# One tile for all slabs, paired transfers of slabs 1+2 and 4+5, and tables through ScalarE's ring in a rotary-embedding kernel

## The chip, the cores and the metric

The kernel runs on one core of one Trainium2 chip. The core has TensorE (matmul), VectorE, ScalarE and GpSimd as compute engines, SyncE, and 16 DMA engines that move data between the device memory (HBM) and the on-chip memory (SBUF, 128 partitions). Each engine works through its own list of instructions in order; an instruction may wait for a semaphore that another engine or a transfer raises. The metric is the time of one execution on the device in microseconds (us), as the median over several executions.

## What is computed

A rotary position embedding. `x` has 16 batches, 512 positions and 1024 values, which are 16 heads of 64; `cos` and `sin` are 512 x 32. All are float32, and the output is 16 x 512 x 16 x 64 in float32.

```python
x = x.reshape(batch, seq, num_heads, head_dim)
x1, x2 = x[..., :half_dim], x[..., half_dim:]
cos = cos[None, :, None, :]
sin = sin[None, :, None, :]
rotated = np.concatenate([
    x1 * cos - x2 * sin,
    x1 * sin + x2 * cos
], axis=-1)
```

Input and output are 33.55 MB each.

## The kernel before

The work is cut into eight slabs of two batches. A slab is 1024 rows of 1024 values, laid on 128 partitions with 8 rows each (`rpp`): 32 KB of float32 per partition (`W` = 8192 values), 4.19 MB in all. One load on SyncE's queue (line 62) brings a slab in; five slab buffers (`slots`) exist, and slab s + 5 is loaded into the buffer of slab s once slab s has been stored. A load of a full slab is 128 rows of 32 KB that are spread over the 16 DMA engines, so each gets 8.

A slab goes through these steps, whole for slabs 1 to 5 and in two halves (passes of four rows per partition) for slabs 0, 6 and 7:

- ScalarE casts it to bfloat16 into `xb` (line 119; two such buffers).
- VectorE multiplies `xb` by the sin table into `t2`, which lies in the first half of the slab's own buffer (line 140), multiplies `xb` by the cos table in place (line 140 again), and adds the two with the halves of each head exchanged (line 143).
- ScalarE casts the sum back to float32 into the slab's buffer (line 146).
- ScalarE issues the store from its own queue (line 158 for slabs 0 to 6; slab 7 is stored in two halves by line 155).

The code asks for the cast of the next pass before the work of the present one. The order on each engine is settled when the program is built. Before the change, ScalarE's order is: casts of slab 0 (two halves), cast of slab 1, both casts back of slab 0, store 0, cast 2, back 1, store 1, cast 3, back 2, store 2, and so on; VectorE finishes one slab's three operations before it begins the next slab's, except that the two halves of slab 0 overlap by one.

The tables are made at the start. Two GpSimd-issued transfers (line 73) bring `cos` and `sin` to 128 partitions, four positions each, in one tile `raw`. GpSimd casts it to bfloat16 (line 98) and builds selection matrices of 1 and -1 (`pick`, lines 89 to 92); eight matmuls (line 104) spread the four-position rows to the eight rows of each partition and sign the sin half; VectorE casts the result from PSUM to `tab` (line 110). VectorE's first multiply needs `tab` and the first cast.

Loads 1 to 4 carry a hand-made dependency on the cos transfer: SyncE issues them only when it has landed. Slab 7's second half has a hand-made order behind the issue of its first half.

Of the kernel before, what the change touches and what calls it, by code (L numbers as in the profile page):

```python
# [2 lines left out]

# [4 lines left out]


@with_exitstack  # L10
def kernel(
    ctx: ExitStack,
    tc: tile.TileContext,
    x: bass.AP,
    cos: bass.AP,
    sin: bass.AP,
    num_heads: int,
    out: bass.AP,
):
    nc = tc.nc  # L20
    P = nc.NUM_PARTITIONS

    batch, seq, dim = x.shape
    nh = num_heads
    hd = dim // nh
    half = hd // 2
    bf16 = mybir.dt.bfloat16
    f32 = mybir.dt.float32

    nb = 2  # L30
    slots = 5
    nslabs = batch // nb
    rpp = nb * seq // P
    W = rpp * dim
    SP = seq // rpp
    TW = rpp * half

    out_flat = out.rearrange("b s h d -> b s (h d)")

    singles = ctx.enter_context(tc.tile_pool(name="singles", bufs=1))  # L40
    slabs = ctx.enter_context(tc.tile_pool(name="slabs", bufs=slots))
    xpool = ctx.enter_context(tc.tile_pool(name="xpool", bufs=2))
    psum = ctx.enter_context(tc.tile_pool(
        name="psum", bufs=1, space=bass.MemoryType.PSUM))


    def dram(t, s, a=0, n=W):
        return bass.AP(tensor=t.tensor, offset=t.offset + s * nb * seq * dim + a,
                       ap=[[W, P], [1, n]])


    def view(t, offset, *dims):
        return dataclasses.replace(t, offset=t.offset + offset,
                                   ap=[t.ap[0], *[list(d) for d in dims]])


    slab = {}


    def load(s):  # L60
        slab[s] = slabs.tile([P, W], f32, tag="slab", name="slab")
        return nc.sync.dma_start(out=slab[s], in_=dram(x, s))  # L62


    load(0)


    TR = seq // P
    G = rpp // TR
    table = {}  # L70
    raw = singles.tile([P, 2 * TR * half], f32, tag="raw")
    for i, src in enumerate((cos, sin)):
        table[i] = nc.gpsimd.dma_start(out=view(raw, i * TR * half, (1, TR * half)), in_=bass.AP(  # L73
            tensor=src.tensor, offset=src.offset,
            ap=[[TR * half, P], [1, TR * half]]))

    for s in range(1, slots):
        tc.add_manual_dep(  # L80
            load(s).ins, table[0].ins.name,
            mybir.DependencyInfo(mybir.DependencyClass.Sync,
                                 mybir.DependencyReason.DATA),
            reason="issue")

    pick = singles.tile([P, 2 * G * P], bf16, tag="pick")
    nc.gpsimd.memset(pick, 0.0)  # L89
    for g in range(2 * G):  # L90
        part = view(pick, g * P, (SP, P // SP), (1, SP))
        nc.gpsimd.affine_select(  # L92
            out=part, in_=part, compare_op=mybir.AluOpType.not_equal,
            fill=1.0 if g < G else -1.0, base=-(g % G),
            pattern=[[0, P // SP], [-G, SP]], channel_multiplier=1)

    tab1 = singles.tile([P, 2 * TR * half], bf16, tag="tab1")
    nc.gpsimd.tensor_copy(out=tab1, in_=raw)  # L98

    acc = psum.tile([P, 2 * rpp * hd], f32, tag="acc")  # L100
    for i in range(2):
        for h in range(2):
            for g in range(G):
                nc.tensor.matmul(  # L104
                    view(acc, (i * rpp + g * TR) * hd + h * half, (hd, TR), (1, half)),
                    view(pick, (i * h * G + g) * P, (1, P)),
                    view(tab1, i * TR * half, (half, TR), (1, half)),
                    start=True, stop=True)
    tab = singles.tile([P, 2 * rpp * hd], bf16, tag="tab")
    nc.vector.tensor_copy(out=tab, in_=acc)  # L110

    xb = {}


    def cast(u):
        s, r, n = u
        if r == 0:
            xb[s] = xpool.tile([P, W], bf16, tag="xb", name="xb")
        nc.scalar.copy(out=view(xb[s], r * dim, (1, n * dim)),  # L119
                       in_=view(slab[s], r * dim, (1, n * dim)))  # L120

    passes = []
    for s in range(nslabs):
        n = rpp if 1 <= s < nslabs - 2 else rpp // 2
        passes += [(s, r, n) for r in range(0, rpp, n)]


    cast(passes[0])
    for i, (s, r, n) in enumerate(passes):
        if i + 1 < len(passes):
            cast(passes[i + 1])
        xs = view(slab[s], r * dim, (1, n * dim))
        xu = view(xb[s], r * dim, (1, n * dim))

        t2 = view(slab[s].bitcast(bf16), 2 * r * dim, (1, n * dim))
        for t, a in ((t2, rpp * hd), (xu, 0)):
            nc.vector.tensor_mul(  # L140
                out=t, in0=xu,
                in1=view(tab, a + r * hd, (hd, n), (0, nh), (1, hd)))
        nc.vector.tensor_add(  # L143
            out=xu, in0=xu, in1=view(t2, half, (hd, n * nh), (-half, 2), (1, half)))

        back = nc.scalar.copy(out=xs, in_=xu)  # L146
        if s == nslabs - 1:

            if r > 0:
                tc.add_manual_dep(  # L150
                    back.ins, part.ins.name,
                    mybir.DependencyInfo(mybir.DependencyClass.NoSync,
                                         mybir.DependencyReason.DATA),
                    reason="issue")
            part = nc.scalar.dma_start(
                out=dram(out_flat, s, r * dim, n * dim), in_=xs)
        elif r + n == rpp:
            nc.scalar.dma_start(out=dram(out_flat, s), in_=slab[s])  # L158
            if s + slots < nslabs:
                load(s + slots)  # L160


# [1 line left out]
_INS = ['x', 'cos', 'sin', 'num_heads']  # L164
_OUTS = [((16, 512, 16, 64), 'float32')]

_NUMBERS = {'num_heads': 16}


# [26 lines left out]
```

## Time and profile before

| | us |
|---|---|
| median of 10 runs (162.25 to 162.75) | 162.44 |
| the profiled execution | 162.48 |
| its span, first to last instruction | 160.7 |
| ScalarE busy | 113.5 |
| VectorE busy | 108.5 |
| cast of a whole slab, ScalarE (line 119) | 7.02 |
| cast back of a whole slab, ScalarE (line 146) | 7.01 |
| each cast of half a slab, ScalarE | 3.60 |
| each VectorE operation on a whole slab (lines 140, 143) | 4.42 |
| each VectorE operation on half a slab | 2.29 |
| load of a slab, issue to landing, median of 8 | 24.1 |
| store of a slab, issue to landing, median of 7 | 28.3 |
| cos and sin, issue to landing | 6.9 and 8.9 |

The span is 1.8 us shorter than the time of the same execution: some time lies around the instructions. The profile tells when each instruction ran, what it waited for, and how busy the 16 DMA engines were; "DMA share" is their mean busy share. Of 67.24 MB moved, 33.69 MB are read from HBM and 33.55 MB written to it. SyncE's queue took 49.3% and ScalarE's 48.4% of the DMA engines' time over the span; GpSimd's took 0.2%.

### The profile page before, as it was taken

The page shows a single profiled execution, that of the slowest core. Times are in us where ns is not written, and L with a number is a line of the kernel's source. Part 1 is how long each engine was busy: PE and PEld are TensorE (multiplying, and loading weights), DVE is VectorE, ACT ScalarE, POOL GpSimd, SP SyncE. Part 2 cuts the span into 40 slices and gives each one's busy share as a digit, 9 for nine tenths or more (in the row PEclk, how much of TensorE's full clock was granted, in tenths as well). Part 3 has the DMA queues.
Part 4 walks back from the last instruction along what each step waited for, and adds up shares of the span by engine and source line. Part 5 has one row for each costly group of instructions (what it writes and reads, how often), then busy time and mean ns, then how long its engine had stood idle before and what let it go on. Part 6 is the DMA issues. An engine that isn't in the chain of part 4 may idle for free.

```text
span 160.7 us, 169 instructions
## 1 busy us (share of the span) xinstructions
PE 1.0 (1%) x8; PEld 0.8 (1%) x8; DVE 108.5 (68%) x34; ACT 113.5 (71%) x23; POOL 3.4 (2%) x12
## 2 busy tenths in 40 slices
PE   0010000000000000000000000000000000000000
PEld 0010000000000000000000000000000000000000
DVE  0003799999899979997995199939469599900000
ACT  3007939998998999899909995199995999280000
POOL 7000000000000000000000000000000000000000
DMA  7999999999999999999999999999999999999994
GB/s 261 408 408 408 506 392 400 506 400 392 383 400 465 440 400 416 489 400 408 498 400 408 498 400 400 506 400 400 498 408 392 489 424 392 473 432 400 416 432 196
DMA packets 2512, 67.24 MB, mean 418 GB/s; under 512 B 304, under 2 KB 304, under 8 KB 336
## 3 DMA queue, kind: packets, MB, share of 16 engines
q1 hardware_dynamic: 1152, 33.55, 49.3%
q10 hardware_dynamic: 1296, 33.56, 48.4%
q0 software_dynamic: 64, 0.13, 0.2%
HBM read 33.69 MB, written 33.55 MB: 418 GB/s over the span
## 4 chain that ended last, share of the span: by engine, by line
DMA 49%; ACT 30%; issue 6%; DVE 4%; ACTq 0%; SPq 0%; POOLq 0%
DMA slab<-in_x_dram 24%; DMA out_dram<-slab 21%; ACT slab L146 16%; ACT xb L119 14%; DMA raw<-in_cos_dram 4%; DVE xb L143 1%; DVE xb L140 1%; DVE slab L140 1%; ACTq L158 0%; SPq L62 0%; POOLq L177 0%
## 5 line engine op out<-in xcount | busy, mean ns | idle before, releaser
L119 ACT CAST xb<-slab 128x4096 bf16<-128x4096 f32 (+1 forms) x11 | 56.6, 5155 | 26.8 <-DMA slab<-in_x_dram 25.6
L146 ACT CAST slab<-xb 128x4096 f32<-128x4096 bf16 (+1 forms) x11 | 56.6, 5153 | 3.4 <-DVE xb L143 3.4
L140 DVE TENSOR_TENSOR slab<-xb,tab 128x4096 bf16<-128x4096 bf16 (+1 forms) x11 | 35.9, 3260 | 19.3 <-ACT xb L119 19.2
L143 DVE TENSOR_TENSOR xb<-xb,slab 128x4096 bf16<-128x4096 bf16 (+1 forms) x11 | 35.9, 3261 | 0.3
L140 DVE TENSOR_TENSOR xb<-xb,tab 128x4096 bf16<-128x4096 bf16 (+1 forms) x11 | 35.9, 3261 | 0.3
L110 DVE CAST tab<-acc 128x1024 bf16<-128x1024 f32 x1 | 1.2, 1225 | 12.4 <-PE acc L104 12.4
L119 ACT ACT_TABLE_LOAD x1 | 1.3, 1283 | 0.7 <-PEq L177 0.7
L104 PE MATMUL acc<-tab,pick 128*128 128x128 bf16 x8 | 1.0, 308 | 11.3 <-POOL tab L98 11.3
L92 POOL TENSOR_SCALAR_AFFINE_SELECT pick<-pick 128x128 bf16<-128x128 bf16 x4 | 1.0, 288 | 0.1
L104 PEld LDWEIGHTS <-pick 128*128 128x128 bf16 x8 | 0.8, 140 | 11.2 <-issue 7.8
L73 POOL DMA_DIRECT2D raw<-in_cos_dram x1 | 0.7, 674 | 0.8 <-POOLq L177 0.8
L89 POOL MEMSET pick<- 128x512 bf16 x1 | 0.5, 543 | 0.0
L98 POOL CAST tab<-raw 128x256 bf16<-128x256 f32 x1 | 0.4, 396 | 6.8 <-DMA raw<-in_sin_dram 6.8
L73 POOL DMA_DIRECT2D raw<-in_sin_dram x1 | 0.5, 534 | 0.0
L177 POOL MEMSET const-float32-0.0<- 128x1 f32 x1 | 0.1, 99 | 0.2 <-issue 0.2
L177 POOL MEMSET const-bfloat16-1.0<- 128x1 bf16 x1 | 0.1, 102 | 0.0
L177 POOL MEMSET const-uint8-127<- 128x1 uint8 x1 | 0.1, 102 | 0.0
L177 POOL MEMSET const-float32-1.0<- 128x1 f32 x1 | 0.1, 99 | 0.0
## 6 DMA issues: line engine op xcount, KB each, us to landing
slab<-in_x_dram SPq DMA_DIRECT2D x8, 4096.0 KB, 24.1
out_dram<-slab ACTq DMA_DIRECT2D x7, 4096.0 KB, 28.3
out_dram<-slab ACTq DMA_DIRECT2D x2, 2048.0 KB, 16.2
raw<-in_cos_dram POOLq DMA_DIRECT2D x1, 64.0 KB, 6.9
raw<-in_sin_dram POOLq DMA_DIRECT2D x1, 64.0 KB, 8.9
```

Source lines behind the costliest of these rows:

```text
L73: table[i] = nc.gpsimd.dma_start(out=view(raw, i * TR * half, (1, TR * half)), in_=bass.AP(tensor=src.tensor, offset=src.offset, ap=[[TR * ...
L89: nc.gpsimd.memset(pick, 0.0)
L92: nc.gpsimd.affine_select(out=part, in_=part, compare_op=mybir.AluOpType.not_equal, fill=1.0 if g < G else -1.0, base=-(g % G), pattern=[[ ...
L98: nc.gpsimd.tensor_copy(out=tab1, in_=raw)
L104: nc.tensor.matmul(view(acc, (i * rpp + g * TR) * hd + h * half, (hd, TR), (1, half)), view(pick, (i * h * G + g) * P, (1, P)), view(tab1, ...
L110: nc.vector.tensor_copy(out=tab, in_=acc)
L119: nc.scalar.copy(out=view(xb[s], r * dim, (1, n * dim)), in_=view(slab[s], r * dim, (1, n * dim)))
L140: nc.vector.tensor_mul(out=t, in0=xu, in1=view(tab, a + r * hd, (hd, n), (0, nh), (1, hd)))
L143: nc.vector.tensor_add(out=xu, in0=xu, in1=view(t2, half, (hd, n * nh), (-half, 2), (1, half)))
L146: back = nc.scalar.copy(out=xs, in_=xu)
L177: nc = _bacc.Bacc("TRN2", target_bir_lowering=False, num_devices=1)
```

## The change

- The five slab buffers become one tile `mem` of five slots. Slab s lies in slot (s + 1) mod 5: slab 0 in slot 1, slabs 1 and 2 in slots 2 and 3, slab 3 in slot 4, slab 4 in slot 0, slab 5 in slot 1.
- Slabs 1 and 2 are loaded by one transfer of 8.39 MB. Slabs 4 and 5 are stored by one transfer of 8.39 MB, issued after slab 5's cast back.
- The last slab is stored by one transfer, after its second half.
- Tables: `cos` and `sin` go to 64 partitions, eight positions (1 KB) each, in two tiles, issued by ScalarE ahead of its other work. GpSimd casts each on its own; four matmuls instead of eight spread and sign them.
- Loads 1 to 4 no longer wait for the cos transfer.

```diff
--- before.py
+++ after.py
@@ -38,15 +38,9 @@
     out_flat = out.rearrange("b s h d -> b s (h d)")
 
     singles = ctx.enter_context(tc.tile_pool(name="singles", bufs=1))
-    slabs = ctx.enter_context(tc.tile_pool(name="slabs", bufs=slots))
     xpool = ctx.enter_context(tc.tile_pool(name="xpool", bufs=2))
     psum = ctx.enter_context(tc.tile_pool(
         name="psum", bufs=1, space=bass.MemoryType.PSUM))
-
-
-    def dram(t, s, a=0, n=W):
-        return bass.AP(tensor=t.tensor, offset=t.offset + s * nb * seq * dim + a,
-                       ap=[[W, P], [1, n]])
 
 
     def view(t, offset, *dims):
@@ -54,58 +48,65 @@
                                    ap=[t.ap[0], *[list(d) for d in dims]])
 
 
-    slab = {}
 
 
-    def load(s):
-        slab[s] = slabs.tile([P, W], f32, tag="slab", name="slab")
-        return nc.sync.dma_start(out=slab[s], in_=dram(x, s))
+    mem = singles.tile([P, slots * W], f32, tag="mem")
+
+
+    def at(s):
+        return (s + 1) % slots * W
+
+
+
+    def dram(t, s, n):
+        return bass.AP(tensor=t.tensor, offset=t.offset + s * nb * seq * dim,
+                       ap=[[W, P], [nb * seq * dim, n], [1, W]])
+
+
+    def sbuf(s, n):
+        return view(mem, at(s), (W, n), (1, W))
+
+
+    def load(s, n=1):
+        nc.sync.dma_start(out=sbuf(s, n), in_=dram(x, s, n))
 
 
     load(0)
 
 
-    TR = seq // P
-    G = rpp // TR
-    table = {}
-    raw = singles.tile([P, 2 * TR * half], f32, tag="raw")
-    for i, src in enumerate((cos, sin)):
-        table[i] = nc.gpsimd.dma_start(out=view(raw, i * TR * half, (1, TR * half)), in_=bass.AP(
-            tensor=src.tensor, offset=src.offset,
-            ap=[[TR * half, P], [1, TR * half]]))
+    cos_sb = singles.tile([SP, TW], f32, tag="cos_sb")
+    sin_sb = singles.tile([SP, TW], f32, tag="sin_sb")
+    for t, src in ((cos_sb, cos), (sin_sb, sin)):
+        nc.scalar.dma_start(out=t, in_=bass.AP(
+            tensor=src.tensor, offset=src.offset, ap=[[TW, SP], [1, TW]]))
+
+    load(1, 2)
+    for s in range(3, slots):
+        load(s)
 
 
 
-    for s in range(1, slots):
-        tc.add_manual_dep(
-            load(s).ins, table[0].ins.name,
-            mybir.DependencyInfo(mybir.DependencyClass.Sync,
-                                 mybir.DependencyReason.DATA),
-            reason="issue")
-
-
-
-    pick = singles.tile([P, 2 * G * P], bf16, tag="pick")
+    pick = singles.tile([SP, 2 * P], bf16, tag="pick")
     nc.gpsimd.memset(pick, 0.0)
-    for g in range(2 * G):
+    for g in range(2):
         part = view(pick, g * P, (SP, P // SP), (1, SP))
         nc.gpsimd.affine_select(
             out=part, in_=part, compare_op=mybir.AluOpType.not_equal,
-            fill=1.0 if g < G else -1.0, base=-(g % G),
-            pattern=[[0, P // SP], [-G, SP]], channel_multiplier=1)
+            fill=1.0 - 2.0 * g, base=0, pattern=[[0, P // SP], [-1, SP]],
+            channel_multiplier=1)
 
-    tab1 = singles.tile([P, 2 * TR * half], bf16, tag="tab1")
-    nc.gpsimd.tensor_copy(out=tab1, in_=raw)
+    tab1 = singles.tile([SP, 2 * TW], bf16, tag="tab1")
+    for i, t in enumerate((cos_sb, sin_sb)):
+        nc.gpsimd.tensor_copy(out=view(tab1, i * TW, (1, TW)), in_=t)
 
     acc = psum.tile([P, 2 * rpp * hd], f32, tag="acc")
     for i in range(2):
         for h in range(2):
-            for g in range(G):
-                nc.tensor.matmul(
-                    view(acc, (i * rpp + g * TR) * hd + h * half, (hd, TR), (1, half)),
-                    view(pick, (i * h * G + g) * P, (1, P)),
-                    view(tab1, i * TR * half, (half, TR), (1, half)),
-                    start=True, stop=True)
+            nc.tensor.matmul(
+                view(acc, i * rpp * hd + h * half, (hd, rpp), (1, half)),
+                view(pick, i * h * P, (1, P)),
+                view(tab1, i * TW, (half, rpp), (1, half)),
+                start=True, stop=True)
     tab = singles.tile([P, 2 * rpp * hd], bf16, tag="tab")
     nc.vector.tensor_copy(out=tab, in_=acc)
 
@@ -117,7 +118,7 @@
         if r == 0:
             xb[s] = xpool.tile([P, W], bf16, tag="xb", name="xb")
         nc.scalar.copy(out=view(xb[s], r * dim, (1, n * dim)),
-                       in_=view(slab[s], r * dim, (1, n * dim)))
+                       in_=view(mem, at(s) + r * dim, (1, n * dim)))
 
 
 
@@ -132,10 +133,10 @@
     for i, (s, r, n) in enumerate(passes):
         if i + 1 < len(passes):
             cast(passes[i + 1])
-        xs = view(slab[s], r * dim, (1, n * dim))
+        xs = view(mem, at(s) + r * dim, (1, n * dim))
         xu = view(xb[s], r * dim, (1, n * dim))
 
-        t2 = view(slab[s].bitcast(bf16), 2 * r * dim, (1, n * dim))
+        t2 = view(mem.bitcast(bf16), 2 * (at(s) + r * dim), (1, n * dim))
         for t, a in ((t2, rpp * hd), (xu, 0)):
             nc.vector.tensor_mul(
                 out=t, in0=xu,
@@ -143,19 +144,13 @@
         nc.vector.tensor_add(
             out=xu, in0=xu, in1=view(t2, half, (hd, n * nh), (-half, 2), (1, half)))
 
-        back = nc.scalar.copy(out=xs, in_=xu)
-        if s == nslabs - 1:
+        nc.scalar.copy(out=xs, in_=xu)
+        if r + n == rpp:
 
-            if r > 0:
-                tc.add_manual_dep(
-                    back.ins, part.ins.name,
-                    mybir.DependencyInfo(mybir.DependencyClass.NoSync,
-                                         mybir.DependencyReason.DATA),
-                    reason="issue")
-            part = nc.scalar.dma_start(
-                out=dram(out_flat, s, r * dim, n * dim), in_=xs)
-        elif r + n == rpp:
-            nc.scalar.dma_start(out=dram(out_flat, s), in_=slab[s])
+            if s != 4:
+                first, count = (4, 2) if s == 5 else (s, 1)
+                nc.scalar.dma_start(out=dram(out_flat, first, count),
+                                    in_=sbuf(first, count))
             if s + slots < nslabs:
                 load(s + slots)
```

In the changed program as built, ScalarE's order is: the two table issues, two half casts of slab 0, two half casts back, store 0, cast 1, cast 2, back 1, store 1, cast 3, back 2, store 2, cast 4, back 3, store 3, cast 5, back 4, two half casts of slab 6, back 5, store 4 and 5, first half back of 6, first half cast of 7, second half back of 6, second half cast of 7, store 6, two halves back of 7, store 7. VectorE's first multiply of slab 2 stands ahead of slab 1's add, and both first multiplies of slab 6's halves ahead of its others. SyncE's list is load 0, loads 1 and 2, 3, 4, and then 5, 6 and 7, which wait for stores 0, 1 and 2.

## The prediction

> **What bounds the kernel now.** I read the page's busy rows and its DMA row first, then the stretches by time, then the chain of waits, then the rows by shape for durations.
>
> ```profile
> PE 1.0 (1%) x8; PEld 0.8 (1%) x8; DVE 108.5 (68%) x34; ACT 113.5 (71%) x23; POOL 3.4 (2%) x12
> DMA  7999999999999999999999999999999999999994
> DMA 49%; ACT 30%; issue 6%; DVE 4%; ACTq 0%; SPq 0%; POOLq 0%
> ```
>
> No compute engine is above 71%, while the DMA row is at 9 in 38 of 40 slices. The chain names transfers for only 49%, but a chain follows one releaser at a time. The stretches show the resource itself:
>
> ```profile
> 0.00:1.70 1.70, 0.00 (x0) 0.00 (x0) 0.00 (x0) 0.96 (x1) 0.67 (x5) 1.00 0.00 0
> 2.00:36.00 34.00, 1.01 (x8) 0.85 (x8) 20.27 (x9) 20.20 (x6) 2.39 (x7) 1.00 0.99 424
> 36.00:44.00 8.00, 0.00 (x0) 0.00 (x0) 7.62 (x2) 7.55 (x2) 0.00 (x0) 1.00 1.01 389
> 66.00:100.00 34.00, 0.00 (x0) 0.00 (x0) 27.75 (x7) 27.88 (x4) 0.00 (x0) 1.00 1.00 433
> 100.00:158.00 58.00, 0.00 (x0) 0.00 (x0) 32.42 (x14) 35.36 (x9) 0.00 (x0) 1.00 1.00 430
> ```
>
> The last two columns are the DMA share and GB/s. From 1.7 us to the end the share is 1.0 for loads alone, loads with stores, and stores alone. So the kernel takes the time its bytes need, and anything that leaves the transfer engines without queued work for a moment is paid in full. One 4.19 MB slab costs 4.194 / 0.4325 = 9.70 us (slabs 1's and 0's casts start 22.93 - 13.22 = 9.71 us apart, each released by its load). The stretch 36 to 44, where the first store begins, is slower: 8 x (1 - 389/430) = 0.8 us lost. The last store is issued at 144.54 and lands 15.0 us later, at 159.5, 1.2 us before the end of the span.
>
> What keeps the queue filled is ScalarE and VectorE, which hand out stores early enough:
>
> ```profile
> 16.86 2.29 DVE L140 TENSOR_TENSOR slab<-xb,tab 128x4096 bf16<-128x4096 bf16 x1 [3.24 <-ACT xb L119]
> 28.11 2.29 DVE L143 TENSOR_TENSOR xb<-xb,slab 128x4096 bf16<-128x4096 bf16 x1
> 29.85 7.11 ACT L146 CAST slab<-xb 128x4096 f32<-128x4096 bf16 x2
> 36.99 0.38 ACTq L158 DMA_DIRECT2D out_dram<-slab  x1
> 51.38 0.34 ACTq L158 DMA_DIRECT2D out_dram<-slab  x1
> 65.72 0.34 ACTq L158 DMA_DIRECT2D out_dram<-slab  x1
> ```
>
> Stores come every 65.72 - 51.38 = 14.34 us when ScalarE is not starved (cast 7.02, cast back 6.93, issue 0.4). A slab needs 2 x 9.70 = 19.4 us of transfer, so ScalarE has slack, but only as long as each store is issued when its own slab is done.
>
> **What the Trainium skill says.** "DMA: Bandwidth & Descriptors", section "Issuing engines are not separate DMA queues": transfers issued by different engines run on the same 16 DMA engines and interleave. The trace agrees: two queues together reach 430 to 433 GB/s, one alone 430. So moving the tables to ScalarE's queue buys no bandwidth. Section "Why a DMA increments its semaphore by 16 and not by 1" says that the number of engines is the largest divisor up to 16 of the slowest dimension: 64 rows still use all 16, four rows each; no run here shows it yet. Section "Queues, rings and completion order" says that each DMA engine takes turns between queues by packet; the cos table in the trace landed 6.9 us after its issue though it is 64 KB, which fits waiting behind slab packets. The section on the increment by 16 also says that only the full count means that all data has landed, and a paired load has one count, so slab 1 is released together with slab 2.
>
> **The change, part by part.**
>
> Tables. Two GpSimd issues (0.67 and 0.53 us) become two ScalarE issues of about 0.35 us, before the activation table load; ScalarE waits until 13.22 for slab 0 anyway, so nothing is paid. Bytes stay 0.13 MB, 0.3 us of all engines. Four 1 KB rows per engine and table, one row for each slab packet of 9.70 / 8 = 1.2 us (8 rows of a slab on each of 16 engines), plus a completion: sin would land about 1.7 + 10 x 1.2 + 0.5 for start-up = 14.2 us as an estimate, against 1.91 + 8.9 = 10.8 now. After it: copy 0.40, two of four matmuls 0.5, tab 1.23, gaps 0.2: ready at 16.7. VectorE needs tab at 16.86. If rows go several at a time, sin lands near 8; if each waits for one more packet, near 15.5, ready at 17.9. Cost D: 0 to 1.0 us (its bytes are the same, so slab 0's landing moves little); I take 0.3.
>
> The removed wait of loads 1 to 4 on cos (SyncE waited 7.0 us) gains nothing: load 0 keeps the transfer engines busy until about 13, the wait ended at 8.1. The removed GpSimd work and four of eight matmuls lay under the wait for slab 0: zero.
>
> Slab 0. ScalarE's order in the built program has both casts back of slab 0 ahead of the cast of slab 1. VectorE ends slab 0 at 28.11 + 2.29 = 30.40; cast back 3.60 to 34.05; store 0 at 34.1, 2.9 us earlier than 36.99. No gain, as the queue holds loads then.
>
> Loads 1 and 2 as one. Both arrive at 13.22 + 2 x 9.71 = 32.6. ScalarE is busy until 34.5, so casting slab 1 starts at 34.5 instead of 22.93. This is the first half of the damage. The second is order: casts of 1 and 2 go back to back (34.5 to 48.5), and VectorE does mul1, mul1, mul2 (of the next slab), and only then the add of slab 1. Four operations of 4.45 from 41.6: 59.4. Cast back 7.0, so store 1 goes at 66.45, against 51.38 before: 15.1 us later. ScalarE stands idle from 48.5 to 59.4 in between. From there ScalarE is without a gap: store 2 at 80.8, store 3 at 95.15.
>
> Stores 4 and 5 as one. Store 4 no longer goes by itself at 95.15 + 14.34 = 109.5; the pair waits for slab 5. After store 3: issue 0.4, cast 5 7.0, back 4 6.95, two half casts of slab 6 (7.1; they now stand ahead of back 5), back 5 7.0: issue at 123.6. VectorE is done with slab 5 at 102.6 + 3 x 4.45 = 116.0, so it is ScalarE that sets this.
>
> What the transfer engines have until then. Load 0 lands at 13.2 with tables and start-up in it; five more loads and two stores are 7 x 9.70 = 67.9, and the first store's slow stretch 0.8, so store 1 lands near 81.9 and the last packet moves about 0.5 earlier. Store 2 is issued at 80.8 + D, load 6 only when store 1 has landed; from issue to first packet is 1.0 us on an empty queue (load 0: issue 0.74, no packet before 1.7). So a first dry spell of 0.4 + D, until 81.8 + D. Then load 6, store 2, store 3, load 7: 38.8, until 120.6 + D. The paired store comes at 123.6 + D, first packet at 124.6 + D: dry for 4.0 us. Left are four slabs, 38.8: 163.4 + D, completion 0.5, and 1.2 to the end: 165.1 + D = 165.4. (The same account for the kernel before, 13.2 + 15 x 9.70 + 0.8 = 159.5, is its last landing.)
>
> Last store whole. Store 6 is issued near 141.7 and store 7 near 152.4 (VectorE's half passes of 2.3, casts of 3.6). The transfer engines need store 7 at 153.7 less 1.0. It comes just in time, since the backlog of the pair covers the later issue; if it is late, by up to 0.5. One fewer issue on ScalarE (0.34) is not on the path.
>
> The persistent tile itself costs nothing: same addresses per pass, same operations, 4.4 and 2.3 us each as in the rows by shape.
>
> Sum: span 160.7 to 165.4, +4.7 (dry spells 0.7 + 4.0). The profiled execution took 162.48, 1.8 above its span, against the median 162.44. So 167.1 us.
>
> **Rivals.**
>
> A, not slower: the backlog still covers the pair. Mechanism: the transfer engines still hold packets when the paired store is issued. It decides at 119.6 + D: if the pair is issued by then, the second dry spell vanishes, and with the first one hidden too the time is that of the bytes, 162.4. For it: ScalarE gains 19.4 - 14.34 = 5.1 us per slab on the transfers. Against it: ScalarE must make up 4 us, and its 57 us from store 1 to the pair contain no wait. Chance 8%, of which 3 for a real gain: were the 0.8 us of the first store's slow stretch gone too, as store 0 now starts under a pair, it would be 161.6.
>
> B, the tables are late: rows of 1 KB wait longer than one packet each, say two; then sin lands near 14.2 + 9 x 1.2 = 25, tab is ready 10 us late, slab 0 shifts and all ScalarE work after it. The loss is direct, since the pair sits at the end of that chain: up to 177; half of it 171. For it: cos took 6.9 us for 64 KB. Against it: that was one packet's wait for data and one for the completion. Chance 7%.
>
> C, the forecast: the pair of loads and the pair of stores delay the stores, and the transfer engines run dry twice. 85%, its own range 166.0 to 168.3: D from 0 to 1, restart of the queue 0.7 to 1.5 us, store 7 late by up to 0.5, the first packets after a dry spell slow, as at the start (load 0 took 13.2 - 1.7 = 11.5 us, 1.8 above 9.70, tables and completion among them).
>
> **Chances.** A run of this kernel can be told from no change at about 0.2%, 0.3 us. Faster 3%, within 5%, slower 92%. Range 165.4 to 168.9: C whole, and the near edges of A (a half dry spell) and B.
>
> **What would show it.** In the profile after: cast of slab 1 starting near 34.5 released by ScalarE or the load; VectorE with three multiplies before slab 1's add; ScalarE idle some 11 us before about 59; store 1 near 66, the pair near 124; DMA slices below 9 near 81 and near 121 to 125; no idle slices after it. It is wrong if the DMA row stays at 9 throughout, if the pair is issued before 120, or if VectorE's first multiply starts later than 18.

## The result

The changed kernel takes 169.42 us (median of 8 runs, 169.13 to 169.58) against 162.46 us for the kernel before (28 runs): a ratio of 1.0426, 95% interval 1.0416 to 1.0435. The profiled execution has a span of 167.3 us against 160.7. The forecast was slower, 167.1 us, range 165.4 to 168.9: the direction and the chain of causes held, the time lies above the range. Ratios leave out runs that took over 1.5% longer than the fastest of their kernel: two of twelve with single loads (166.15 and 166.60 us), two of twelve with the new tables alone (165.54 and 165.68) and one of fifteen of the last version below (167.54), none of the kernel before or of the changed one.

The page of the changed kernel, in the same rows as before:

```profile
PE 1.2 (1%) x4; PEld 0.5 (0%) x4; DVE 107.8 (64%) x34; ACT 113.7 (68%) x23; POOL 1.8 (1%) x9
DMA  7899999999999969999989999999978889898985
ACT 38%; DVE 35%; issue 10%; DMA 7%; ACTq 1%; PE 0%; POOLq 0%; POOL 0%; DVEq 0%
sin_sb<-in_sin_dram ACTq DMA_DIRECT2D x1, 64.0 KB, 15.9
```

The engines are as busy as before in microseconds, but the DMA row now has holes, and the chain that ended last names ScalarE and VectorE for 73% and transfers for 7%. It was 34% and 49%. The sin table, issued at 1.30, lands 15.9 us later, at 17.2; before it landed at 10.8.

The timeline of ScalarE (ACT) and VectorE (DVE) shows the delay grow; columns are start, length, engine, line, operation, and in brackets the idle time ahead and its releaser. The first line, on GpSimd (POOL), is the cast of the sin table, the second the cast that finishes the tables:

```profile
17.29 0.39 POOL L100 CAST tab<-sin_sb 64x256 bf16<-64x256 f32 x1 [4.87 <-DMA sin_sb<-in_sin_dram]
18.35 1.22 DVE L111 CAST tab<-acc 128x1024 bf16<-128x1024 f32 x1 [18.35 <-PE acc L105]
19.67 2.29 DVE L141 TENSOR_TENSOR mem<-xb,tab 128x4096 bf16<-128x4096 bf16 x1
36.94 0.34 ACTq L152 DMA_DIRECT2D out_dram<-mem  x1
37.33 13.94 ACT L120 CAST xb<-mem 128x8192 bf16<-128x8192 f32 x2 [0.41 <-ACT mem L147]
44.38 4.42 DVE L141 TENSOR_TENSOR mem<-xb,tab 128x8192 bf16<-128x8192 bf16 x1 [11.16 <-ACT xb L120]
48.83 4.43 DVE L141 TENSOR_TENSOR xb<-xb,tab 128x8192 bf16<-128x8192 bf16 x1
53.18 4.42 DVE L141 TENSOR_TENSOR mem<-xb,tab 128x8192 bf16<-128x8192 bf16 x1
57.51 4.42 DVE L144 TENSOR_TENSOR xb<-xb,mem 128x8192 bf16<-128x8192 bf16 x1
62.02 7.02 ACT L147 CAST mem<-xb 128x8192 f32<-128x8192 bf16 x1 [10.76 <-DVE xb L144]
69.07 0.34 ACTq L152 DMA_DIRECT2D out_dram<-mem  x1
126.18 0.39 ACTq L152 DMA_DIRECT2D out_dram<-mem  x1
```

VectorE begins to multiply 2.8 us later than before (19.67 against 16.86), as soon as the late sin table has been cast and spread. The two casts of slabs 1 and 2 start at 37.33, released by ScalarE itself and not by their load, which landed at 33.0. VectorE does three multiplies, the third of slab 2, before slab 1's add, while ScalarE idles for 10.76. Store 1 goes at 69.07 (51.38 before), the paired store at 126.18.

What that does to the transfer engines, in stretches (share and GB/s are the last two columns):

```profile
60.00:64.00 4.00, 0.00 (x0) 0.00 (x0) 4.00 (x2) 1.98 (x1) 0.00 (x0) 1.00 0.80 279
64.00:123.00 59.00, 0.00 (x0) 0.00 (x0) 50.97 (x14) 57.74 (x10) 0.00 (x0) 1.00 0.99 408
123.00:128.00 5.00, 0.00 (x0) 0.00 (x0) 5.00 (x3) 3.15 (x1) 0.00 (x0) 1.00 0.50 216
128.00:165.00 37.00, 0.00 (x0) 0.00 (x0) 17.50 (x8) 21.33 (x6) 0.00 (x0) 1.00 1.02 439
```

The share falls near 62 and near 125: there is no work queued. A stretch counts a packet (one row, 1.2 us) whole where it starts, so a stretch of a few us is rough by up to a packet; by the packets' own starts and lengths in the trace, the transfer engines stand idle for 1.4 us between 61.3 and 63.9 and for 2.3 us between 124.1 and 127.6. Against 430 GB/s, another 59 x (1 - 408/430) = 3.0 us are lost between the two holes, at a share of 0.99: the engines are busy, but some packets take longer. After 128 only stores are left, at full rate, to the end. Summed over the whole span from the packets' own times, the changed kernel has 3.2 us more of idle transfer engines and 3.4 us more of slow packets than the kernel before, which makes up the 6.6 us by which its span is longer.

### The profile page after: what moved, and what is told of

Its sections match the earlier page's. It is cut to its first block, busy times and chain, and to the rows that moved or that the text cites. A ratio compares the mean times of both kernels' runs of the same rounds, so it can differ in the third digit from the quotient of the medians.

```text
span 167.3 us, 154 instructions
## 1 busy us (share of the span) xinstructions
PE 1.2 (1%) x4; PEld 0.5 (0%) x4; DVE 107.8 (64%) x34; ACT 113.7 (68%) x23; POOL 1.8 (1%) x9
## 4 chain that ended last, share of the span: by engine, by line
ACT 38%; DVE 35%; issue 10%; DMA 7%; ACTq 1%; PE 0%; POOLq 0%; POOL 0%; DVEq 0%
ACT mem L147 21%; ACT xb L120 17%; DVE mem L141 15%; DVE xb L141 12%; DVE xb L144 8%; DMA cos_sb<-in_cos_dram 7%; ACTq L152 1%; DVE tab L111 1%; PE acc L105 0%; POOLq L186 0%; POOL tab L100 0%; ACTq L147 0%; DVEq L141 0%
## 5 line engine op out<-in xcount | busy, mean ns | idle before, releaser
L147 ACT CAST mem<-xb 128x4096 f32<-128x4096 bf16 (+1 forms) x11 | 56.7, 5154 | 26.8 <-DVE xb L144 26.8
L120 ACT CAST xb<-mem 128x4096 bf16<-128x4096 f32 (+1 forms) x11 | 56.4, 5154 | 11.9 <-DMA mem<-in_x_dram 10.2
L141 DVE TENSOR_TENSOR mem<-xb,tab 128x4096 bf16<-128x4096 bf16 (+1 forms) x11 | 35.8, 3259 | 24.1 <-ACT xb L120 23.9
L144 DVE TENSOR_TENSOR xb<-xb,mem 128x4096 bf16<-128x4096 bf16 (+1 forms) x11 | 35.8, 3258 | 0.2
L105 PE MATMUL acc<-tab,pick 64*128 64x256 bf16 x4 | 1.2, 392 | 17.1 <-POOL tab L100 17.1
L93 POOL TENSOR_SCALAR_AFFINE_SELECT pick<-pick 64x128 bf16<-64x128 bf16 x2 | 0.5, 287 | 0.1
L105 PEld LDWEIGHTS <-pick 64*128 64x128 bf16 x4 | 0.5, 112 | 17.4 <-issue 15.9
## 6 DMA issues: line engine op xcount, KB each, us to landing
sin_sb<-in_sin_dram ACTq DMA_DIRECT2D x1, 64.0 KB, 15.9
```

The lines of the kernel that those rows point to most:

```text
L93: nc.gpsimd.affine_select(out=part, in_=part, compare_op=mybir.AluOpType.not_equal, fill=1.0 - 2.0 * g, base=0, pattern=[[0, P // SP], [-1 ...
L105: nc.tensor.matmul(view(acc, i * rpp * hd + h * half, (hd, rpp), (1, half)), view(pick, i * h * P, (1, P)), view(tab1, i * TW, (half, rpp) ...
L120: nc.scalar.copy(out=view(xb[s], r * dim, (1, n * dim)), in_=view(mem, at(s) + r * dim, (1, n * dim)))
L141: nc.vector.tensor_mul(out=t, in0=xu, in1=view(tab, a + r * hd, (hd, n), (0, nh), (1, hd)))
L144: nc.vector.tensor_add(out=xu, in0=xu, in1=view(t2, half, (hd, n * nh), (-half, 2), (1, half)))
```

## The experiments

Theory 1 is the forecast's: the paired load and the order that comes with it make all stores late, the paired store sets when the last four slabs may begin, and what delays slab 0 adds to that one for one. The rivals blame single parts by themselves. Each run names what it changes against the changed kernel or the kernel before.

**Old tables in the changed kernel** (GpSimd's queue, 128 partitions, loads behind cos):

```diff
-    for t, src in ((cos_sb, cos), (sin_sb, sin)):
-        nc.scalar.dma_start(out=t, in_=bass.AP(
...
+    for i, src in enumerate((cos, sin)):
+        table[i] = nc.gpsimd.dma_start(out=view(raw, i * TR * half, (1, TR * half)), in_=bass.AP(
...
```

> The changed kernel with the tables brought in as before (GpSimd's queue, 128 partitions, eight matmuls, later loads waiting for cos). Theory 1 (the tables' lateness shifts ScalarE's whole chain one for one): VectorE's first multiply at 16.9 instead of 19.67, paired store issued near 123.4 instead of 126.18, time 169.4 - 2.8 = 166.6 us. Rival 2 (the paired load alone sets when slab 1 starts, so late tables are covered): 169.0 to 169.5 us.

166.78 us, ratio 1.0266 (1.0251 to 1.0282). Paired store at 123.47. The late tables cost 2.6 us in the changed kernel; rival 2 falls.

**Single loads for slabs 1 and 2**:

```diff
-    load(1, 2)
-    for s in range(3, slots):
+    for s in range(1, slots):
```

> The changed kernel with slabs 1 and 2 loaded by two transfers; new tables, paired store and whole last store stay. Theory 1 (the paired load makes the stores late, and the paired store only hurts on top of that): store 1 near 54, paired store near 118 to 121 while load 7 still runs, no dry spell of the DMA engines, 162.3 to 163.2 us. Rival 3 (the paired store by itself empties the DMA queue): at least 165 us.

162.42 us, ratio 1.0 (0.9983 to 1.0017): all of the loss is gone, and rival 3 falls. Its timeline and two of its stretches:

```profile
19.96 2.29 DVE L140 TENSOR_TENSOR mem<-xb,tab 128x4096 bf16<-128x4096 bf16 x1
37.69 0.34 ACTq L151 DMA_DIRECT2D out_dram<-mem  x1
53.84 0.34 ACTq L151 DMA_DIRECT2D out_dram<-mem  x1
118.89 0.39 ACTq L151 DMA_DIRECT2D out_dram<-mem  x1
...
2.00:120.00 118.00, 1.16 (x4) 0.35 (x3) 91.22 (x27) 92.27 (x17) 0.79 (x2) 1.00 1.00 429
120.00:158.00 38.00, 0.00 (x0) 0.00 (x0) 16.82 (x8) 21.33 (x6) 0.00 (x0) 1.00 0.99 427
```

VectorE starts as late as in the changed kernel, yet store 0 goes at 37.69, only 0.7 us later than before the change: slab 1's cast, again ahead of the casts back, had delayed store 0 anyway. The paired store is still there, issued at 118.89, but load 7 is still running, and the share stays at 1.00. So neither late tables, nor the paired store, nor the whole last store costs anything while the stores flow.

**Single stores for slabs 4 and 5**:

```diff
-            if s != 4:
-                first, count = (4, 2) if s == 5 else (s, 1)
-                nc.scalar.dma_start(out=dram(out_flat, first, count),
-                                    in_=sbuf(first, count))
+            nc.scalar.dma_start(out=dram(out_flat, s, 1), in_=sbuf(s, 1))
```

> The changed kernel with slabs 4 and 5 stored by two transfers; new tables, paired load and whole last store stay. Theory 1: store 4 goes near 112 instead of 126, the dry spell of 2.3 us near 125 vanishes, the one near 61 and the slow packets stay: 169.4 - 2.3 = 167.1 us. Rival 4 (all of the loss lies in the paired load, the gap near 125 is made up elsewhere): 169.4. Rival 3 (the paired store is the loss): 163 us.

168.45 us, ratio 1.0376 (1.0342 to 1.0411). A gain of 1.0, not 2.3; rival 4, no gain at all, lies just outside the interval. Store 4 goes at 112.15 and the hole near 125 is gone, but the backlog that the pair had built up is gone too, and the last store, issued whole at 154.01, now comes after the queue has run empty:

```profile
140.00:152.00 12.00, 0.00 (x0) 0.00 (x0) 9.96 (x5) 8.44 (x3) 0.00 (x0) 1.00 1.01 437
152.00:156.00 4.00, 0.00 (x0) 0.00 (x0) 0.00 (x0) 1.98 (x1) 0.00 (x0) 1.00 0.65 279
156.00:164.00 8.00, 0.00 (x0) 0.00 (x0) 0.00 (x0) 0.00 (x0) 0.00 (x0) 1.00 1.07 459
```

By the packets' own times the engines stand idle there for 0.7 us, and the hole near 62 is longer in this execution, 1.8 us against 1.4: of the 2.3 us gained near 125, 1.2 are lost again. The expectation was wrong in taking a hole's length for its price.

**New tables alone**, in the persistent tile, with the loads, stores and last halves of before:

> Only the new tables and the single persistent tile; loads and stores one slab each, last slab stored in halves. Theory 1: VectorE starts 2.8 us late here too, store 0 near 39.8 instead of 37.0, but the DMA engines have loads queued until after 60, so 162.5 us, as before the change. Rival 5 (a late start of VectorE costs its own length everywhere): 165.3 us.

162.16 us, ratio 0.9984 (0.9972 to 0.9995). Store 0 at 37.60, not 39.8: the delay of 2.8 us is covered once more by slab 1's cast. Rival 5 falls, and the persistent tile, which this run has too, costs nothing beside the new tables.

**Tables in SyncE's ring behind load 0** (a ring is the list of transfers that one engine has issued), all else as changed:

```diff
-        nc.scalar.dma_start(out=t, in_=bass.AP(
+        nc.sync.dma_start(out=t, in_=bass.AP(
```

> The changed kernel with the two table transfers issued by SyncE behind load 0 instead of by ScalarE: same rows, same bytes, another ring. Theory 1 (each 1 KB row in ScalarE's ring waits behind slab packets of SyncE's ring): rows follow load 0 back to back, sin lands near 13.8 instead of 17.2, VectorE's first multiply at 16.9 to 17.2, paired store near 123.6, 166.8 us. Rival 6 (64 small rows are slow in themselves): VectorE near 19.7 as in the changed kernel, 169.4 us.

166.53 us, ratio 1.0254 (1.0239 to 1.0269). The same rows and bytes now end the casts of both tables at 14.5 and leave VectorE waiting for ScalarE only:

```profile
13.79 0.39 POOL L100 CAST tab<-cos_sb 64x256 bf16<-64x256 f32 x1 [12.15 <-DMA cos_sb<-in_cos_dram]
14.13 0.39 POOL L100 CAST tab<-sin_sb 64x256 bf16<-64x256 f32 x1
17.01 2.29 DVE L141 TENSOR_TENSOR mem<-xb,tab 128x4096 bf16<-128x4096 bf16 x1 [0.51 <-ACT xb L120]
123.55 0.39 ACTq L152 DMA_DIRECT2D out_dram<-mem  x1
```

Rival 6 falls.

**512 B rows in ScalarE's ring**, twice as many, with the one table tile and the eight matmuls of the kernel before:

```diff
-            tensor=src.tensor, offset=src.offset, ap=[[TW, SP], [1, TW]]))
...
+            tensor=src.tensor, offset=src.offset,
+            ap=[[TR * half, P], [1, TR * half]]))
...
```

> The changed kernel with tables of 128 rows of 512 B in ScalarE's ring (and the eight matmuls that belong to them): same bytes, twice the rows. Theory 1 (one row for each slab packet of 1.2 us): first row at 5.9 as now, then 8 + 1 + 8 steps of 1.25, sin lands near 27.7 instead of 17.2, VectorE starts near 30, paired store near 136.7, 180 us. Rival 7 (the bytes and a fixed delay of the second queue set it): sin near 17, 169.4 us.

176.71 us, ratio 1.088 (1.0864 to 1.0896), 7.3 us above the changed kernel. sin landed 23.1 us after its issue at 1.16, at 24.3, not 27.7; VectorE began at 27.23 and the paired store went at 133.75. Rival 7 falls: the number of rows sets it. The DMA counts by stretch show how. First the changed kernel, up to 5.5 us and from 5.5 to 6.8 us, queue by queue (packets, MB, share); q1 is SyncE's ring here and q10 ScalarE's:

```profile
DMA packets 48, 1.57 MB, mean 286 GB/s; under 512 B 0, under 2 KB 0, under 8 KB 0
q1 hardware_dynamic: 48, 1.57, 77.4%
...
DMA packets 32, 0.54 MB, mean 416 GB/s; under 512 B 0, under 2 KB 16, under 8 KB 16
q1 hardware_dynamic: 16, 0.52, 93.3%
q10 hardware_dynamic: 16, 0.02, 3.5%
```

By 5.5 us the 16 DMA engines have started 48 slab packets, three each, and no table row, although cos was issued at 0.73. In the next 1.3 us each starts one slab packet and one row of 1 KB. From 6.8 to 8 it is 16 and 16 again. The same two stretches in the run with 512 B rows, up to 2.9 and from 2.9 to 4.2:

```profile
DMA packets 16, 0.52 MB, mean 181 GB/s; under 512 B 0, under 2 KB 0, under 8 KB 0
q1 hardware_dynamic: 16, 0.52, 64.5%
...
DMA packets 32, 0.53 MB, mean 410 GB/s; under 512 B 0, under 2 KB 16, under 8 KB 16
q1 hardware_dynamic: 16, 0.52, 93.3%
q10 hardware_dynamic: 16, 0.01, 2.3%
```

The first row came two packets earlier here, after one slab packet (cos took 0.40 us to issue, against 0.53). That is 2.4 us of the 3.4 by which the expectation of 27.7 was off; why the first row waits for three packets in one run and one in the other was not tried. From then on it is again one row for one slab packet. "DMA: Bandwidth & Descriptors" of the Trainium skill, section "Queues, rings and completion order", says that an engine takes turns between queues by packet, and that a packet holds typically some 9 to 17 descriptors. The turns are seen here; in these rings a turn of the table was one row.

**The order alone**: VectorE's first multiply of slab 2 held behind slab 1's add.

```diff
+            if s == 2 and a > 0:
+                tc.add_manual_dep(
+                    mul.ins, add.ins.name,
...
-        nc.vector.tensor_add(
+        add = nc.vector.tensor_add(
```

> The changed kernel with VectorE's first multiply of slab 2 held behind slab 1's add (order alone). Theory 1 (the order costs store 1, and all after it, one 4.4 us operation): store 1 near 64.6 instead of 69.1, paired store near 121.8, no dry spell left near 125, after which the transfers bound it at 167.3 - 2.3 = 165.0 us of span, 166.8 to 167.1 us. Rival 8 (ScalarE makes the order up within the next slabs): 169.4 us.

165.72 us, ratio 1.0215 (1.0166 to 1.0264), 3.7 below the changed kernel (runs of 165.16 to 167.13), so rival 8 falls. Store 1 at 65.09, paired store at 122.76 (a wait of 0.6 for load 6 came in). One line of order is worth about half of the loss. The reason given beforehand was only in part right: the hole near 125 did not vanish but shrank (the last line below, 8 x (1 - 0.83) = 1.4 us), and the end is still set by the paired store, not by the transfers:

```profile
53.53 4.42 DVE L150 TENSOR_TENSOR xb<-xb,mem 128x8192 bf16<-128x8192 bf16 x1
57.87 4.42 DVE L141 TENSOR_TENSOR mem<-xb,tab 128x8192 bf16<-128x8192 bf16 x1
58.04 7.02 ACT L153 CAST mem<-xb 128x8192 f32<-128x8192 bf16 x1 [6.55 <-DVE xb L150]
...
120.00:128.00 8.00, 0.00 (x0) 0.00 (x0) 7.78 (x4) 5.12 (x2) 0.00 (x0) 1.00 0.83 356
```

**The paired load alone**, on the kernel before, with the persistent tile that it needs:

> Only the paired load (and the persistent tile): tables, stores and last store as in the kernel before. Theory 1 (the paired load costs only by what it leaves the transfer engines without): store 0 at 34.2, store 1 at 66.4, no dry spell, 162.5 to 163.0 us. Rival 9 (where one direction runs alone and the other joins it, packets become slow, with no dry spell needed): about 2 us of slow packets as in the run with the old tables, 164.5 us.

165.25 us, ratio 1.0164 (1.0136 to 1.0192). Store 0 and 1 at 34.35 and 66.51 as expected, but the time is 2.8 us above the kernel before: theory 1 as written here, with no loss expected, is wrong, and rival 9 comes close. Its stretches tell where:

```profile
34.00:42.00 8.00, 0.00 (x0) 0.00 (x0) 0.18 (x1) 7.55 (x3) 0.00 (x0) 1.00 1.01 393
79.00:84.00 5.00, 0.00 (x0) 0.00 (x0) 4.97 (x2) 4.59 (x2) 0.00 (x0) 1.00 0.83 354
84.00:90.00 6.00, 0.00 (x0) 0.00 (x0) 5.00 (x2) 6.00 (x2) 0.00 (x0) 1.00 1.02 360
96.00:106.00 10.00, 0.00 (x0) 0.00 (x0) 8.96 (x3) 10.00 (x2) 0.00 (x0) 1.00 0.99 410
```

In the kernel before, the same four stretches have 393, 426, 437 and 423 GB/s. Against 430, the new losses are 5 x (1 - 354/430) = 0.9 us, where the share falls to 0.83 and the queue is short of work, then 1.0 and 0.5 at a full share: packets that take longer. By the packets' own times these are 0.4 us of idle engines near 81, and 1.2 and 0.4 of slow packets; another 0.6 us lie at the end, where the 16 engines run out of work less evenly than before. The slow packets after 84 come just when load 6 joins a store that had run alone. I read both kinds of loss as the work of the late stores, which leave one direction alone more often; no run tests this by itself.

**A pair whose slabs are not wanted early**: the kernel before with slabs 3 and 4 as one transfer.

```diff
-    for s in range(1, slots):
+    for s, n in ((1, 1), (2, 1), (3, 2)):
```

> The kernel before with one persistent tile in which slabs 3 and 4 (not 1 and 2) lie side by side and come by one transfer of 8.39 MB; all else as before. Theory 1 (a paired load costs only where its first slab is wanted before its second has come): the pair lands near 64.7, slab 3's cast is due at 66.1, so no step moves: 162.3 to 162.7 us. Rival 10 (a transfer of two slabs is slow in itself or upsets the mix of the two directions): 164 us or more, as with slabs 1 and 2 (165.25).

162.12 us, ratio 0.998 (0.9969 to 0.999), a little under the expected range. Rival 10 falls: a transfer of 8.39 MB is not slow in itself. My reason was wrong, though: 66.1 is when slab 4's cast is due, slab 3's is due at 52.2, and ScalarE did wait:

```profile
51.78 0.34 ACTq L169 DMA_DIRECT2D out_dram<-mem  x1
63.65 7.02 ACT L128 CAST xb<-mem 128x8192 bf16<-128x8192 f32 x1 [11.91 <-DMA mem<-in_x_dram]
77.62 0.34 ACTq L169 DMA_DIRECT2D out_dram<-mem  x1
```

Store 2 goes 11.9 us later than before, and nothing is lost: stores 0 and 1 had gone on time, and the transfer engines are never idle for lack of work until the end. Store 2 going 12 us late is free; store 1 going 15 us late, as with slabs 1 and 2 paired, is not.

**The last store**, in halves, beside single stores and in the changed kernel:

> The new tables and the paired load, single stores of 4 and 5, and the last slab stored in halves. Theory 1 (in the run with single stores the whole last store came 0.7 us too late for the transfer engines, the paired store's backlog hides that in the changed kernel): first half of the last store near 147, no gap near 154, 168.45 - 0.7 = 167.7 us. Rival 11 (the form of the last store never matters): 168.4 us.

> The changed kernel with the last slab stored in two halves. Theory 1 (end = issue of the paired store + 41.1 us, whatever the last store looks like): 169.3 to 169.6 us. Rival 12 (the whole last store costs the 0.7 us that it cost beside single stores): 168.7 us.

167.85 us (1.0291 to 1.0352) and 169.72 us (1.0429 to 1.0458). In the first the rate from 152 to 156 is 385 GB/s instead of 279, and by the packets' own times that hole is gone. The gain of 0.6 is about the expected 0.7, but the two intervals overlap, and the two profiled executions (168.06 and 168.10 us) have the same span, 166.3: whether halves gain anything is not settled. In the second, halves gain nothing (169.72 against 169.42, 0.1 above the expected range): with the paired store's backlog the form of the last store does not matter, and rival 12 falls.

**The version that the runs point to**: single loads and stores, halves at the end, the 64-row tables in SyncE's ring behind load 0.

> The version that the runs point to: kernel before with the 64-row tables issued by SyncE behind load 0, no wait for cos, one slab per load and store. Theory 1 (transfers bind, tables are in time, nothing to gain but the tables' small cost): 162.0 to 162.4 us. Rival 13 (the removed wait and tables out of the other ring save the start's slow packets too): 161.6 us or less.

162.21 us, ratio 0.9985 (0.9977 to 0.9994), as theory 1 has it. It is 7.2 us better than the changed kernel, and 0.15% better than the kernel before, less than the 0.2% named as telling; rival 13 falls. The new tables alone and the pair of slabs 3 and 4 are 0.16% and 0.2% better. There is no clear gain over the kernel before in any run.

## Why the prediction was right in kind and wrong in size

The end of the changed kernel is the issue of the paired store and a constant. With that store at 126.18, 123.47, 123.55, 122.76 and 133.75 (changed; old tables; SyncE's ring; order; 512 B rows) the spans are 167.3, 164.8, 164.7, 163.9 and 174.9: 41.1 to 41.3 us later each time. The forecast had 165.4 - 123.9 = 41.5. The issues in the three runs that were not shown above (old tables, order, 512 B rows):

```profile
123.47 0.39 ACTq L165 DMA_DIRECT2D out_dram<-mem  x1
122.76 0.39 ACTq L158 DMA_DIRECT2D out_dram<-mem  x1
133.75 0.39 ACTq L157 DMA_DIRECT2D out_dram<-mem  x1
```

- **Bound, order and chain: right.** Store 0 to store 1 was forecast as 66.45 - 34.1 = 32.35 and measured as 69.07 - 36.94 = 32.13; store 1 to the pair 57.15, measured 57.11; ScalarE's idle stretch 11, measured 10.76. "mul1, mul1, mul2 (of the next slab), and only then the add of slab 1" was read from the instruction order, and the run that undoes this gives 3.7 us of the loss back.
- **The step that failed: the tables, "Cost D: 0 to 1.0 us ... I take 0.3".** D, the delay of VectorE's first multiply, was 2.8 us, and the forecast's own sign of being wrong, a first multiply later than 18, came true at 19.67. The sum "1.7 + 10 x 1.2 + 0.5" let the first row move with the first slab packet at 1.7. It moved at 5.9, after three slab packets: 4.2 us that the sum did not have. One row for each slab packet was right, and the steps were about right: from the first row to the landing of sin the sum has 12.5 us, the trace 11.3. Twice the rows made it 7 us later, and with the rows behind load 0 in the same ring D was 0.15. With D = 2.8 in the forecast's own sum, 167.1 + 2.5 = 169.6, against 169.42. That it comes so near is no proof of the sum's dry spells: the end hangs on the paired store. The trace of before had shown this lead: the first store was issued at 36.99, its first packet moved at 41.0, and it landed 24.5 us after its issue, where two interleaved slabs need 19.4; I used 1.2 us steps without it. Rival B named the late tables, but as two packets per row.
- **Why D counts here and nowhere else.** In the runs with single loads VectorE starts as late and nothing is lost. In the changed kernel slab 1's casts stand behind slab 0's casts back on ScalarE, so slab 0's delay runs through to the paired store.
- **The dry spells: a little too long, the first in the wrong place, and not the whole loss.** Forecast 0.7 near 81 and 4.0 near 125, 4.7; measured 1.4 near 62 and 2.3 near 125, 3.7, and about 3 more between them in slow packets. Of these the forecast had only slow first packets after a dry spell, in the range of its case C; by the packets' own times they are 0.6 us, when load 5 starts alone at 63, and 2.5 us lie later, mostly where store 1 and load 6 join. The first dry spell moved because store 0, late by D, landed when the first five loads were through (load 5 was issued at 62.08). With SyncE's ring and with the paired load alone, where D is small, it is near 81 as forecast, 0.7 and 0.4 us. D alone doesn't fix its place: with single stores and halves, where D is 3.0, it is 0.3 us near 62 and 2.4 near 83. The slow packets shortened the wait at 125 instead of adding to the end, as ScalarE's chain, not the transfers, set the paired store.
- **Rival A (backlog covers) failed in the changed kernel** for the reason given: the pair went at 126.18, the transfers were done near 124. It is what happens once the loads are single: pair at 118.89, no loss.
- **Persistent tile, whole last store, removed wait for cos: cost nothing, right**; for the whole last store this is shown with a paired store, and open with single stores.

## What to carry to other kernels

In a kernel bound by transfers, ask of each change when the transfer queue could run empty, and follow the slab that feeds it: here a pair that delays the first stores cost 2.8 us by itself and 7.0 with the rest of the change, and a pair two slabs later cost none. Read the instruction order of the built program before summing: the cost of the paired load was in what it moved on ScalarE and VectorE more than in its own landing. A small transfer beside bulk traffic in another ring was priced here by its rows times the bulk packet's time, and by the packets that stand ahead of its first row; behind the load that is wanted first, in that load's own ring, it came within 1 us of it.

## What was unexpected in the hardware

- A second ring's first row moved only after one to three 32 KB packets (1.2 us each) of the ring that had started first, and then one row went for each such packet, whether of 1 KB or of 512 B. The same 128 rows of 1 KB behind a slab in its own ring were through within 1 us of that slab (the casts of cos and sin began at 13.79 and 14.13, that of slab 0 at 13.38).
- Where a direction (loads or stores) joins one that has run alone, packets were often slow for some microseconds at a full share: 356 GB/s from 68 to 76 and 352 from 88 to 92 in the changed kernel, 360 from 84 to 90 with the paired load alone. The slow ones are mostly those of the direction that was running, before the other one's first packet moves: loads that start from 71 to 74 took 1.80 us instead of 1.21, with store 1's first packet at 73.0; stores that start from 88 to 91 took 1.93, with load 6's first at 90.0. Not every join is slow. Where store 0 joins, 0.8 to 0.9 us were lost in the kernel before, with the old tables and with the paired load alone, 0.5 in the changed kernel and with slabs 3 and 4 paired, and 0.1 or less with single loads, with the new tables alone, with SyncE's ring and in the last version. What decides it was not tried.
